# A decoder step's first stage: order of its loads, where x is normalised, which engines split weights, and a shorter block of index queries

## The chip, the core and the metric

The kernel runs on one core of a Trainium2 chip. The core has a matrix engine (TensorE, PE in the profile, with its weight loads as PEld), three engines for elementwise work (VectorE, ScalarE and GpSimd: DVE, ACT and POOL) and SyncE (SP), which here only issues transfers. Each engine runs its own list of instructions in order; they wait for one another through semaphores. Data lies in SBUF (128 partitions) and PSUM (where matmuls accumulate), and comes from HBM by DMA. The metric is the time of one execution on the device in microseconds; less is better.

## The reference

One step of a decoder layer for 1024 new prompt tokens and 8 x 4 sample tokens (32), 1056 columns together, with D = 1024. Cut to what matters:

```python
mod = silu(c) @ w_ada + b_ada                  # (1 + 8 conditions) x 3072
shift, scale, gate = split(mod, 3)
h = x * rsqrt(mean(x*x) + EPS) * g_norm * (1 + scale) + shift
qa, ka, va, za, qi, ki, wi, qr, kr, vr, zr, ga, gr = split(h @ w_in)
# index scores: 4 heads of 64; each query token picks its 256 best keys
s = einsum('bqhd,bsd->bqhs', qi, ki)
scores = einsum('bqhs,bqh->bqs', relu(s), wi * 0.0625)
idx = top_k(where(key <= query, scores, -inf), 256)
y_a = attention of qa over the picked rows of ka, va;  y_a *= silu(za)
y_r = group_norm(retention(rotary(qr), rotary(kr), vr)) * g_ret * silu(zr)
x = x + gate * ((sigmoid(ga) * (y_a @ w_pa) + sigmoid(gr) * (y_r @ w_pr)) @ w_out)
y = rms_norm(x, g_final)
```

The sample tokens see 1024 cached keys, found through a page table, beside their own four. A prompt token below 256 has at most 256 admissible keys, so all of them are taken and its scores decide nothing. The rows of k, v and the index keys and the retention states are outputs too.

## The kernel before, in words

*Numbers.* All products of `h @ w_in` are made in three terms. Each fp32 operand is split in a high part in the reduced format fp32r and the rest: `HH`, `HL` for h, `wh`, `wl` for a weight block. `terms` (L206 to L210) issues, for one row block k of eight and one piece of columns, `wh*HH` (L208), `wh*HL` (L209) and `wl*HH` (L210). The 1056 columns go in three pieces of 352 (`chunks`). A block of 128 output features is thus 3 x 8 x 3 = 72 matmuls.

*Order.* The code is written in a framework that takes each instruction in program order, tracks what it reads and writes, and then orders each engine's list by its own estimates; so work of a later stage may stand among the work of an earlier one. `tc.issue_after(i)` keeps what stands under it behind instruction i. Transfers of SyncE are issued in the order of its list. A pool's `bufs=n` says how many tiles of a name exist; the n+1st waits until the first one is free.

*The head* (L231 to L339) makes HH and HL. The constants C (L146), the 32 sample rows and the eight blocks of 128 rows of x (`x_load`, L253) and the blocks of w_ada (`load_wa`, L320; 16 blocks of 1024 x 128, 512 KB each, in five buffers, a shift and a scale block for each k) come through SyncE. `cond` makes silu(c) transposed. `x_blocks` takes the nine row blocks in three groups of three: sums of squares on ScalarE (L284), an inverse square root by integer start and three Newton steps on VectorE, each x scaled by its factor on VectorE or GpSimd (L291), eight transposes on TensorE (L294) and two copies, one on ScalarE and one on VectorE, into XR, which holds x transposed (L296). `h_tile(k)` then makes shift and scale for 128 features: 2 x 8 small matmuls with the w_ada blocks (`ada_rows`, L198 to L202), a copy (L304), two more small matmuls that add the four partial rows (L307), AA and BB on VectorE (L308, L309), h = XR * AA + BB (L311, the 32 sample columns in two operations at L314), HH as a cast on ScalarE (L315) and HL as the difference, on GpSimd for k = 2, 4, 6 and on VectorE otherwise (L316).

`start_two` (L214 to L226) projects the first two feature blocks, the index keys (KI, with the four index weights behind them) and the first half of the index queries (QI), while HH and HL come: six PSUM banks (2 blocks x 3 pieces) are accumulated over k. Their weights are split on GpSimd (L221, L222).

*Behind the head.* `project` (L356) makes any other block; `prefetch` (L351) loads and splits the next one ahead: cast to wh on ScalarE (L194), wl on GpSimd when the number of blocks left is a multiple of three and on VectorE otherwise (L195). Two buffers each (`wp`). The first prefetched block is the second half of QI. Its results and the first half's go to QS by `use_qi`, those of KI to KH and KL by `use_ki`. The index scores follow: for the row blocks b = 7 down to 2, products of QS with KH and KL (L644, L645), relu on ScalarE (L647), the weighted sum over heads on VectorE (L649, L651) into SC[b]; then the sample rows with gathered cached keys into SCS (L711).

*The selection* (L727 and what follows) searches for each row the threshold of its 256 best keys: VectorE counts entries above a candidate (L727), ScalarE does so for block 7 and the sample rows (L734), and small operations move the candidates (L741 to L747, L803, L805). In the end the picked keys are written as a mask BI (L779 to L783: comparison, running count, choice, mask). Under this stage TensorE makes the retention: for each of four pairs of heads (`pair`) the projections of k, q, v and z, and states S over eight chunks of 128 tokens, seven dependent steps on VectorE (L488), read by TensorE at L507; between the pairs come blocks of the attention queries and of the gates. Then follow the attention keys and values, the attention over masked scores, the output projections and the last norm.

## Time and profile before

| | us |
|---|---|
| median of three runs | 1189.28 (1185.84 to 1189.39) |
| the profiled execution | 1189.59 |
| span in the profile | 1187.8 |
| TensorE busy | 1108.8 (93% of the span), 8040 matmuls |
| VectorE busy | 664.8 (56%) |
| ScalarE busy | 454.3 (38%) |
| GpSimd busy | 329.7 (28%) |
| HBM | 149 GB/s over the span |

A busy time says only that an instruction was under way; which engine sets the time of a stage is told by its waits. A row of the waits names the waiting engine with its tile and line, behind the arrow the engine, tile and line that it waited for, and then the us in all, how many times, and the longest. In a row of the timeline stand start, duration, engine, line, operation, output and inputs with their shapes, and in brackets the idle time before it and what ended it; "x28" means that 28 alike in a row are put together. In a row of the windows stand the length, the busy time (and count) of TensorE's matmuls and weight loads, VectorE, ScalarE and GpSimd, then the granted TensorE clock (1 is full), the mean busy share of the DMA engines and GB/s.

### The profile page before, as it was taken

The page shows a single profiled execution, that of the slowest core. Times are in us where ns is not written, and L with a number is a line of the kernel's source. Part 1 is how long each engine was busy: PE and PEld are TensorE (multiplying, and loading weights), DVE is VectorE, ACT ScalarE, POOL GpSimd, SP SyncE. Part 2 cuts the span into 40 slices and gives each one's busy share as a digit, 9 for nine tenths or more (in the row PEclk, how much of TensorE's full clock was granted, in tenths as well). Part 3 has the DMA queues.
Part 4 walks back from the last instruction along what each step waited for, and adds up shares of the span by engine and source line. Part 5 has one row for each costly group of instructions (what it writes and reads, how often), then busy time and mean ns, then how long its engine had stood idle before and what let it go on. Part 6 is the DMA issues. An engine that isn't in the chain of part 4 may idle for free. (4 is left out here: it accounts for less than half of the span.)

```text
span 1187.8 us, 20303 instructions
## 1 busy us (share of the span) xinstructions
PE 1108.8 (93%) x8040; PEld 1011.9 (85%) x8040; DVE 664.8 (56%) x1599; ACT 454.3 (38%) x874; POOL 329.7 (28%) x258
## 2 busy tenths in 40 slices
PE   4999999999989959999998999999997999988997
PEld 3899989999889959999998999777976888886786
DVE  6765359999999996023222122100364766586655
ACT  5365455554555202122233332211343656432211
POOL 3413016024212511241321212242132333484000
PEclk9899999999999978999999999999998999999999
DMA  9913244144224323332775776687898551586221
GB/s 308 244 35 105 73 122 129 26 151 119 74 78 127 110 57 113 93 106 65 265 252 177 223 215 185 198 287 245 243 246 230 156 159 46 161 248 186 96 104 54
DMA packets 157892, 181.51 MB, mean 153 GB/s; under 512 B 18837, under 2 KB 129501, under 8 KB 156710
## 3 DMA queue, kind: packets, MB, share of 16 engines
q1 hardware_dynamic: 147864, 144.51, 41.5%
q0 software_dynamic: 9856, 35.66, 9.2%
q8 instruction: 63, 1.03, 0.4%
q14 instruction: 31, 0.25, 0.1%
q10 hardware_dynamic: 78, 0.06, 0.0%
HBM read 137.81 MB, written 38.60 MB: 149 GB/s over the span
## 5 line engine op out<-in xcount | busy, mean ns | idle before, releaser
L208 PE MATMUL pj<-hh,wh 128*128 128x352 f32 x1176 | 387.9, 330 | 8.7 <-ACT kx L394 3.7
L210 PE MATMUL pj<-hh,wl 128*128 128x352 f32 x1176 | 382.8, 325 | 0.0
L209 PE MATMUL pj<-hl,wh 128*128 128x352 f32 x1176 | 382.7, 325 | 0.0
L208 PEld LDWEIGHTS pj<-hh,wh 128*128 128x128 f32 x1176 | 223.0, 190 | 18.5 <-issue 6.4
L210 PEld LDWEIGHTS pj<-hh,wl 128*128 128x128 f32 x1176 | 223.2, 190 | 3.9 <-issue 3.4
L209 PEld LDWEIGHTS pj<-hl,wh 128*128 128x128 f32 x1176 | 223.6, 190 | 3.3 <-issue 2.5
L727 DVE TENSOR_SCALAR_CACHE_REDUCE eq<-sc,cand 128x896 bf16<-128x896 f32 (+4 forms) x155 | 135.7, 876 | 2.3
L195 POOL TENSOR_TENSOR wl<-ws,wh 128x1024 fp32r<-128x1024 f32 (+1 forms) x33 | 65.1, 1973 | 187.7 <-ACT wh L194 187.7
L194 ACT CAST wh<-ws 128x1024 fp32r<-128x1024 f32 (+1 forms) x65 | 61.2, 942 | 102.8 <-PE pj L209 66.3
L195 DVE TENSOR_TENSOR wl<-ws,wh 128x1024 fp32r<-128x1024 f32 x32 | 40.0, 1250 | 87.1 <-ACT wh L194 81.2
L1064 POOL TENSOR_SCALAR lg<-lg,st 128x1024 f32<-128x1024 f32 (+7 forms) x64 | 47.4, 746 | 93.4 <-DVE st L1063 83.9
L1062 ACT ACTIVATE lg<-lg,st 128x1024 f32<-128x1024 f32 (+7 forms) x64 | 49.5, 774 | 34.4 <-DVE st L1061 34.1
L734 ACT ACTIVATE ra<-sc,cand 128x1024 bf16<-128x1024 f32 x31 | 35.7, 1151 | 65.1 <-DVE cand L805 65.1
L910 POOL DMA_INDIRECT kv<-in_cache_k,idx x32 | 30.9, 965 | 102.8 <-PE str L940 84.7
L942 DVE COPY kt<-str 128x512 f32<-128x512 f32 x32 | 22.1, 690 | 61.0 <-PE str L940 53.8
L910 POOL DMA_INDIRECT kv<-in_cache_v,idx x32 | 31.7, 992 | 72.4 <-PE sx L968 43.3
L1215 PE MATMUL pj<-woh,MH 128*128 128x512 f32 (+1 forms) x136 | 51.5, 380 | 0.0
L1217 PE MATMUL pj<-woh,ML 128*128 128x512 f32 (+1 forms) x136 | 51.2, 377 | 0.0
L1216 PE MATMUL pj<-wol,MH 128*128 128x512 f32 (+1 forms) x136 | 51.2, 377 | 0.0
L573 ACT ACTIVATE raw<-pj 128x352 f32<-128x352 f32 x48 | 22.1, 460 | 72.5 <-PE pj L210 65.6
L1077 PE MATMUL tr<-C,lg 128*128 128x128 f32 x288 | 43.6, 275 | 0.8 <-DVE pT L1079 0.3
L1057 DVE CUSTOM_DVE_ANT_0 lg<-lg,bi 128x512 f32<-128x512 f32 (+3 forms) x64 | 37.1, 587 | 9.0 <-PE lg L1056 8.4
(337 smaller groups left out, 2054.4 us busy)
## 6 DMA issues: line engine op xcount, KB each, us to landing
ws<-in_w_in SPq DMA_DIRECT2D x51, 512.0 KB
TG<-raw SPq DMA_DIRECT2D x16, 528.0 KB
rot<-in_rot SPq DMA_DIRECT2D x8, 1056.0 KB
wa<-in_w_ada SPq DMA_DIRECT2D x16, 512.0 KB
u<-TG SPq DMA_DIRECT2D x8, 528.0 KB
RT<-u SPq DMA_DIRECT2D x8, 528.0 KB
t<-TG SPq DMA_DIRECT2D x8, 528.0 KB
u<-RT SPq DMA_DIRECT2D x8, 528.0 KB
```

The lines of the kernel that those rows point to most:

```text
L194: nc.scalar.copy(wh[:, :, :n], ws[:, :, :n])
L195: (nc.vector if len(order) % 3 else nc.gpsimd).tensor_sub(wl[:, :, :n], ws[:, :, :n], f32(wh[:, :, :n]))
L208: nc.tensor.matmul(p, wh[:, k], HH[k][:, sl], start=(k == 0), stop=False)
L209: nc.tensor.matmul(p, wh[:, k], HL[k][:, sl], start=False, stop=False)
L210: nc.tensor.matmul(p, wl[:, k], HH[k][:, sl], start=False, stop=(k == KT - 1))
L727: nc.vector.tensor_scalar(junk[:n, :W], sc, thr[:n, j:j + 1], 0.0, op0=op, op1=OP.add, accum_out=cnt[:n, j:j + 1])
L910: nc.gpsimd.indirect_dma_start(out=t.rearrange("p s c -> p (s c)"), out_offset=None, in_=cache.rearrange("g (r s) h d -> (g r) (s h d)", s ...
L1062: nc.scalar.activation(l, l, AF.Exp, bias=st[:, 2:3], scale=0.125, accum_out=st[:, 3:4])
L1064: nc.gpsimd.tensor_scalar(l, l, st[:, 0:1], 0.5, op0=OP.mult, op1=OP.mult)
L1215: nc.tensor.matmul(x, MH[:, k, tk], wh[:, k], start=(k == 0), stop=False)
L1216: nc.tensor.matmul(x, MH[:, k, tk], wl[:, k], start=False, stop=False)
L1217: nc.tensor.matmul(x, ML[:, k, tk], wh[:, k], start=False, stop=(k == KT - 1))
```

## The change

*Loads.* Of C only the first 128 columns, the identity matrix, are loaded first (`C_CAUS` is 128), then the two weight blocks of `start_two`, then x, then the rest of C, then w_ada. The w_ada blocks go into the buffers of the x pool (11 of 4 KB per partition), shift and scale block of a k together. The prefetched w_in blocks stand behind the last w_ada load (`tc.issue_after(loads[-1].ins)`).

*Weights of `start_two`.* They are split by ScalarE (cast) and VectorE (difference) rather than GpSimd. The loop interleaves the banks term by term, and QI has two pieces of 400 columns (256 to 655 and 656 to 1055, `late`) in the place of three of 352; the second half of QI has the same. So there are five banks rather than six.

*x.* `x_block` transposes the raw rows as they come and takes the sum of squares beside it, on VectorE for t = 1 and 4 and on ScalarE otherwise; the squares themselves go into the tile BI[7], which is free then (BI and BIS are allocated earlier for it). `norms` runs for the blocks 0 to 4 and 5 to 8 of SEQ: the inverse square roots, then for each block of 128 tokens a diagonal matrix of them, multiplied with a matrix of ones, which gives each factor in all partitions (RB). The 32 sample columns are scaled at once.

*h.* `modulation` is the first part of the old `h_tile`. AA and the prompt's shift are made on ScalarE, with g_norm * (1 + ...) folded in as scale and bias (`cg`). h = XT * AA * RB in one operation on VectorE; the shift is added in the cast to HH on ScalarE as its bias, and again in the operation that makes HL, which is always on VectorE. The samples' shifts are added before, less the prompt's shift.

GpSimd has no work left in the head, save a share of the low parts of prefetched weights (L195), as before.

```diff
...
-SQD = ()
+SQD = (1, 4)
...
-GRP = (0, 3, 6, 9)
-CP = 0
-PH = (2, 4, 6)
...
-    nc.sync.dma_start(C, A["cst"])
+    nc.sync.dma_start(C[:, :C_CAUS], A["cst"][:, :C_CAUS])
...
+    BI = {b: selp.tile([128, (b + 1) * 128], BF, name=f"bi{b}") for b in range(8)}
+    BIS = selp.tile([NS, LK], BF, name="bis")
...
-            nc.tensor.matmul(x[32 * q:32 * q + 32], scT[:, k], w[:, k], start=(k < 4), stop=(k >= 4))
+            nc.tensor.matmul(x[32 * q:32 * q + 32], scT[:, k], w(k), start=(k < 4), stop=(k >= 4))
...
-    def start_two(pool, f0, f1):
-
-        banks = [pj()[:, :CH] for _ in (0, 1)] + [x[:, o:o + CH] for x in (pl(), pl()) for o in (0, 512)]
-        W = []
-        for f in (f0, f1):
-            ws = wload(wp, w_in, f, 128)
-            wh, wl = [pool.tile([128, KT, 128], F32R, name="x", bufs=9) for _ in "hl"]
-            nc.gpsimd.tensor_scalar(wh, ws, 1.0, 1.0, op0=OP.mult, op1=OP.mult)
-            nc.gpsimd.tensor_sub(wl, ws, f32(wh))
-            W.append((wh, wl))
+    late = [slice(256, 656), slice(656, TT)]
+
+    def start_two(W):
+
+        x, y = pl(), pl()
+        parts_ = [(p[:, :sl.stop - sl.start], sl, i) for p, sl, i in
+                  zip((pj(), pj(), x[:, :512], x[:, 512:], y[:, :512]), chunks + late, (0, 0, 0, 1, 1))]
         for k in range(KT):
-            for i, p in enumerate(banks):
-                terms(p, W[i // 3], k, chunks[i % 3])
-        return banks
+            for term in range(3):
+                for p, sl, i in parts_:
+                    nc.tensor.matmul(p, W[i][term == 2][:, k], (HL if term == 1 else HH)[k][:, sl],
+                                     start=(k == 0 and term == 0), stop=(k == KT - 1 and term == 2))
+        return [p for p, sl, i in parts_]
...
-        NWA = 5
-        warm = sp.tile([1, 1], F32, name="warm")
...
+        ssq = sp.tile([128, 12], F32, name="ssq")
+        nc.vector.memset(ssq, 1.0)
...
+        part = lambda: sp.tile([128, D], F32, name="x", bufs=11)
+        W = []
+        for f in (O_KI, O_QI):
+            ws = wload(wp, w_in, f, 128)
+            wh, wl = [sp.tile([128, KT, 128], F32R, name="w", bufs=4) for _ in "hl"]
+            nc.scalar.copy(wh, ws)
+            nc.vector.tensor_sub(wl, ws, f32(wh))
+            W.append((wh, wl))
+        craw, th = [part()[:9] for _ in (0, 1)]
...
-        rows = sp.tile([48, 128], F32, name="rows")
+        rows = sp.tile([128, 128], F32, name="dg", bufs=3)[:48]
...
+        cg = cols[:, 36:44]
+        one = sp.tile([128, 128], F32, name="one")
+        nc.vector.memset(one, 1.0)
+        XT = sp.tile([128, KT, TT], F32, name="xt")
+        RB = sp.tile([128, TT], F32, name="rb")
...
-            X[t] = sp.tile([128, D], F32, name="x", bufs=9)
-            nc.sync.dma_start(X[t][:n], xp[t * 128:t * 128 + 128] if t < 8 else xs)
+            X[t] = part()
+            nc.sync.dma_start(X[t][:size(t)], xp[t * 128:t * 128 + 128] if t < 8 else xs)
...
+            nc.vector.tensor_tensor(cg, cols[:, 8:16], cols[:, 24:32], op=OP.mult)
...
-        def x_blocks(i0, i1):
...
+        def x_block(i):
+
+            t = SEQ[i]
+            n, x = size(t), X[t]
+            p = pl().rearrange("p (k t) -> p k t", k=KT)
+            for k in range(KT):
+                nc.tensor.transpose(p[:, k, :n], x[:n, 128 * k:128 * k + 128], ident[:n, :n])
+            sq = BI[7]
+            if t in SQD:
+                nc.vector.tensor_tensor_reduce(out=sq[:n], in0=x[:n], in1=x[:n], scale=1.0, scalar=0.0,
+                                               op0=OP.mult, op1=OP.add, accum_out=ssq[:n, i:i + 1])
+            else:
+                nc.scalar.activation(sq[:n], x[:n], AF.Square, accum_out=ssq[:n, i:i + 1])
+            for g, copy in ((slice(0, 4), nc.scalar.copy), (slice(4, 8), nc.vector.tensor_copy)):
+                copy(XT[:, g, t * 128:t * 128 + n], p[:, g, :n])
+
+        def norms(i0, i1):
+
             v = sp.tile([128, i1 - i0], F32, name="vv", bufs=2)
             nc.vector.tensor_scalar(v, ssq[:, i0:i1], 1.0 / D, EPS, op0=OP.mult, op1=OP.add)
             r = rsqrt(sp, v, i1 - i0)
-            for i in range(i0, i1):
-                t = SEQ[i]
-                n, x = size(t), X[t]
-                (nc.vector if t % 2 else nc.gpsimd).tensor_scalar(x[:n], x[:n], r[:n, i - i0:i - i0 + 1], 1.0, op0=OP.mult, op1=OP.mult)
...
-        def h_tile(k, w2):
+            p, c0 = pt(), 128 * SEQ[i1 - 4]
+            for i in range(i1 - 4, i1):
+                dg = sp.tile([128, 128], F32, name="dg", bufs=3)
+                nc.vector.tensor_scalar(dg, ident, r[:, i - i0:i - i0 + 1], None, op0=OP.mult)
+                o = 128 * (i - i1 + 4)
+                nc.tensor.matmul(p[:, o:o + 128], one, dg, start=True, stop=True)
+            nc.scalar.copy(RB[:, c0:c0 + 512], p)
+            if i0 == 0:
+                p = pt()
+                dg = sp.tile([128, 128], F32, name="dg", bufs=3)
+                nc.vector.tensor_scalar(dg[:NS, :NS], ident[:NS, :NS], r[:NS, 0:1], None, op0=OP.mult)
+                nc.tensor.matmul(p[:, :NS], one[:NS], dg[:NS, :NS], start=True, stop=True)
+                nc.vector.tensor_tensor(XT[:, :, T:], XT[:, :, T:], p[:, :NS].unsqueeze(1).to_broadcast([128, KT, NS]), op=OP.mult)
+
+        def modulation(k):
...
-            for o, w in enumerate(w2):
-                ada_rows(pm[:, 128 * o:128 * o + 128], w)
+            for o in (0, 1):
+                ada_rows(pm[:, 128 * o:128 * o + 128], lambda c: wa[k][o][:, c])
...
-            nc.vector.tensor_scalar(AA[:, k], pm[:, 16:25], cols[:, 8 + k:9 + k], cols[:, 24 + k:25 + k], op0=OP.add, op1=OP.mult)
-            nc.vector.tensor_scalar(BB[:, k], pm[:, 0:9], cols[:, k:k + 1], None, op0=OP.add)
...
-            nc.vector.tensor_scalar(h, h, AA[:, k, 0:1], BB[:, k, 0:1], op0=OP.mult, op1=OP.add)
...
-            for op, ab in ((OP.mult, AA), (OP.add, BB)):
-                nc.vector.tensor_tensor(hs, hs, ab[:, k, 1:9].unsqueeze(2).to_broadcast([128, NB, NI]), op=op)
-            nc.scalar.copy(HH[k], XR[:, k])
-            (nc.gpsimd if k in PH else nc.vector).tensor_tensor(HL[k], XR[:, k], f32(HH[k]), op=OP.subtract)
...
-            nc.sync.dma_start(wa[j], wcols(A["w_ada"][0], KT, (j % 2) * 1024 + (j // 2) * 128, 128))
...
+        def h_tile(k, pm):
+
+            shift = BB[:, k, 0:1]
+            nc.scalar.activation(AA[:, k], pm[:, 16:25], AF.Identity, bias=cg[:, k:k + 1], scale=cols[:, 24 + k:25 + k])
+            nc.scalar.activation(shift, pm[:, 0:1], AF.Identity, bias=cols[:, k:k + 1])
+
+            nc.vector.tensor_scalar(BB[:, k, 1:9], pm[:, 1:9], cols[:, k:k + 1], shift, op0=OP.add, op1=OP.subtract)
+            h = XT[:, k]
+            nc.vector.scalar_tensor_tensor(h[:, :T], h[:, :T], AA[:, k, 0:1], RB[:, :T], op0=OP.mult, op1=OP.mult)
+            hs = h[:, T:].rearrange("p (b i) -> p b i", b=NB)
+            by_seq = lambda ab: ab[:, k, 1:9].unsqueeze(2).to_broadcast([128, NB, NI])
+            nc.vector.tensor_tensor(hs, hs, by_seq(AA), op=OP.mult)
+            nc.vector.tensor_tensor(hs, hs, by_seq(BB), op=OP.add)
+            nc.scalar.activation(HH[k], h, AF.Identity, bias=shift)
+            nc.vector.scalar_tensor_tensor(HL[k], h, shift, f32(HH[k]), op0=OP.add, op1=OP.subtract)
+
+        wa, loads = {}, []
+
+        def load_wa(k):
+
+            wa[k] = [part().rearrange("p (k f) -> p k f", f=128) for _ in (0, 1)]
+            for o, w in enumerate(wa[k]):
+                loads.append(nc.sync.dma_start(w, wcols(A["w_ada"][0], KT, 1024 * o + 128 * k, 128)))
...
-        for j in range(NWA - 2):
-            load_wa(j)
-        for i in range(len(GRP) - 1):
-            if i == CP:
-                cond()
-                for j in range(NWA - 2, NWA):
-                    load_wa(j)
-            x_blocks(GRP[i], GRP[i + 1])
+        nc.sync.dma_start(C[:, C_CAUS:], A["cst"][:, C_CAUS:])
+        cond()
+        for i in range(9):
+            x_block(i)
+            if i == 4:
+                norms(0, 5)
+        norms(5, 9)
         for k in range(KT):
-            h_tile(k, (wa.pop(2 * k), wa.pop(2 * k + 1)))
-            for j in (2 * k + NWA, 2 * k + NWA + 1):
-                if j < 16:
-                    load_wa(j)
-        first = start_two(sp, O_KI, O_QI)
+            load_wa(k)
+            h_tile(k, modulation(k))
+        first = start_two(W)
...
-            split.append((f0, wsplit(wp, wload(wp, w_in, f0, 128), 128)))
-
-    def project(f0, use):
+            with tc.issue_after(loads[-1].ins):
+                ws = wload(wp, w_in, f0, 128)
+            split.append((f0, wsplit(wp, ws, 128)))
+
+    def project(f0, use, chunks=chunks):
...
-            p = pj()[:, :CH]
+            p = pj()[:, :sl.stop - sl.start]
...
-                    sl = slice(c * CH, c * CH + CH)
+                    sl = late[c]
...
-                        if c == 2:
+                        if c == 1:
...
-                                                      src[:, CH - NS:].rearrange("p (b i) -> p b i", b=NB))
+                                                      src[:, T - sl.start:].rearrange("p (b i) -> p b i", b=NB))
...
-            project(O_QI + 128, use_qi(2))
+            project(O_QI + 128, use_qi(2), late)
...
```

34 lines of the change are left out of this document (5 added, 29 removed).

## Prediction

> **What bounds the kernel now.** I read the waits of TensorE first, then windows of 40 us, then the waits and the timeline of VectorE, and last the head in windows of 10 us. TensorE is busy in nearly every slice of the page, so the question is where it waits. Between 60 and 820 us one wait stands out (us in total, times, longest):
>
> ```profile
> PE pl L507 <- DVE S L488: 12.2, 1, 12.2
> ```
>
> The windows show why (length, busy us and count of PE, PEld, DVE, ACT, POOL, then clock, DMA share, GB/s); the first and the last of the seven windows of one stage, and the one behind it:
>
> ```profile
> 180.00:220.00 40.00, 37.58 (x271) 35.67 (x270) 38.30 (x90) 21.75 (x40) 16.81 (x9) 0.96 0.36 108
> ...
> 420.00:460.00 40.00, 27.82 (x187) 26.85 (x186) 38.92 (x58) 4.57 (x9) 0.56 (x1) 0.70 0.18 49
> 460.00:500.00 40.00, 40.00 (x255) 39.72 (x254) 7.78 (x19) 8.51 (x14) 7.43 (x4) 1.00 0.44 131
> ```
>
> From 180 to 460 us VectorE is full (38.3 and 38.9 of 40 us; 7.8 in the next): it searches the thresholds of the top keys (L727 and what follows), and TensorE, which fills the time with projections, runs out of work at 426 and stands still until VectorE has written S for the third pair of retention heads. So up to 438.7 us the path is: head, projections and index scores on TensorE, then VectorE's queue. From there TensorE is again nearly always busy, and the end follows it. VectorE becomes full when ScalarE has counted its first row block:
>
> ```profile
> DVE base L747 <- ACT ra L734: 6.4, 2, 5.9
> ```
>
> ```profile
> 161.61 1.00 ACT L711 COPY scs<-pl 32x1024 f32<-32x1024 f32 x1 [2.65 <-PE pl L709]
> ```
>
> This wait ends at 163.8 us: ScalarE stood until L709 on TensorE had finished. The start of VectorE's stage thus hangs on TensorE's queue, and TensorE's queue on the head:
>
> ```profile
> 36.98 0.92 PE L208 MATMUL pj<-hh,x 128*128 128x352 f32 x2 [1.33 <-ACT hh L315]
> ...
> 43.78 0.33 PE L209 MATMUL pl<-hl,x 128*128 128x352 f32 x1
> ...
> 70.26 0.32 PE L210 MATMUL pl<-hh,x 128*128 128x352 f32 x1
> ```
>
> The first product of the head's projection stands at 36.98; its last (L210 on pl) starts at 70.26 and starts follow each other by 0.16 us, so it ends at 70.4. Up to 43.8 the same products run at about half speed.
>
> **Part by part.** *Index queries from token 256 on.* Each of two column blocks gets 2 pieces of 400 columns for 3 of 352. One block is 72 products before (3 pieces x 8 x 3 terms) and 48 after. TensorE's timeline gives the prices, at half clock behind the long wait and at full clock later:
>
> ```profile
> 438.66 3.25 PE L507 MATMUL pl<-S,qrT 64*128 64x64 f32 x28 [12.18 <-DVE S L488]
> ...
> 449.57 0.49 PE L210 MATMUL pj<-hh,wl 128*128 128x352 f32 x1
> 449.86 0.49 PE L208 MATMUL pj<-hh,wh 128*128 128x352 f32 x1
> ...
> 453.38 0.32 PE L208 MATMUL pj<-hh,wh 128*128 128x352 f32 x1
> 453.54 0.32 PE L209 MATMUL pj<-hl,wh 128*128 128x352 f32 x1
> ```
>
> Full clock: 453.54 - 453.38 = 0.16 us for 352 columns, so 0.182 for 400. 72 x 0.16 = 11.5 and 48 x 0.182 = 8.7: 2.8 us less for the second block, all of it on TensorE's queue ahead of L709. The first block's part lies in the head.
>
> *Order of the projections among the index scores.* The built programs show 301 projection products between the second query block and the last L709 before (144 of the head and 72 of that block not counted) and 278 after. 23 x 0.16 = 3.7 us less stand ahead of VectorE's full stage; they are done behind it, where TensorE has the 12.2 us of slack.
>
> *VectorE's order in front of S.* In the changed program seven operations of the selection have moved ahead of the sixth S step of the third pair (L516 there), which is what TensorE waits for. Their prices stand in the timeline, where they now come behind that step (438.23):
>
> ```profile
> 438.23 0.28 DVE L488 SCALAR_TENSOR_TENSOR S<-S,rc,pt 128x64 f32<-128x64 f32 x1
> ...
> 438.42 0.76 DVE L782 SCALAR_TENSOR_TENSOR ra<-sc,base,ra 128x512 f32<-128x512 f32 x1
> ...
> 439.08 0.56 DVE L779 TENSOR_SCALAR eq<-sc,base 128x640 f32<-128x640 f32 x1
> ...
> 440.17 0.43 DVE L783 TENSOR_SCALAR bi<-ra 128x512 bf16<-128x512 f32 x1
> ...
> 440.63 1.49 DVE L780 TENSOR_TENSOR_SCAN ra<-eq 128x640 f32<-128x640 f32 x1
> ...
> 442.16 0.88 DVE L781 SCALAR_TENSOR_TENSOR ra<-ra,rem,eq 128x640 f32<-128x640 f32 x1
> ...
> 443.08 0.89 DVE L782 SCALAR_TENSOR_TENSOR ra<-sc,base,ra 128x640 f32<-128x640 f32 x1
> ...
> 443.88 0.61 DVE L779 TENSOR_SCALAR eq<-sc,base 128x768 f32<-128x768 f32 x1
> ```
>
> 0.76 + 0.56 + 0.43 + 1.49 + 0.88 + 0.89 + 0.61 = 5.6 us later for S. VectorE has no idle time there to hide them.
>
> *First weights first, w_ada and prefetches last.* SyncE's queue now issues 64 KB of C, two 512 KB blocks of w_in, x, the rest of C, all sixteen w_ada blocks, and only then the prefetched w_in blocks (the new wait of prefetch on the last w_ada load) and ptab. Before, the third w_in block went out behind nine w_ada blocks. On ScalarE the cast of that prefetched block (L193) stands behind the third HH and ahead of AA for k = 3. What waits there: AA, the next sum, HH 3 to 7, and through them VectorE's h and HL and TensorE. Bytes ahead of and in that block: 0.07 + 1.05 + 4.33 + 0.34 + 16 x 0.524 + 0.52 = 14.70 MB. What the transfers moved:
>
> ```profile
> 0.00:10.00 10.00, 0.00 (x0) 0.00 (x0) 1.02 (x7) 4.74 (x7) 0.20 (x4) 1.00 0.82 281
> 10.00:20.00 10.00, 5.29 (x32) 4.95 (x33) 8.52 (x33) 8.57 (x18) 3.67 (x3) 1.00 1.10 350
> 20.00:30.00 10.00, 7.31 (x105) 5.71 (x104) 9.65 (x22) 3.31 (x7) 6.53 (x5) 1.00 1.18 292
> 30.00:40.00 10.00, 8.12 (x112) 6.81 (x111) 9.55 (x18) 5.71 (x9) 4.36 (x4) 0.85 1.14 287
> 40.00:50.00 10.00, 10.00 (x93) 9.26 (x90) 8.86 (x11) 2.83 (x4) 5.27 (x2) 0.81 1.13 291
> ```
>
> 10 us at 281, 350, 292, 287 and 291 GB/s sum to 2.8, 6.3, 9.2, 12.1 and 15.0 MB, so 14.70 MB are moved by 48.9 us. The lag from there to landing, and when ScalarE reaches the cast, come from these rows:
>
> ```profile
> 31.30 1.69 SPq L188 DMA_DIRECT2D ws<-in_w_in  x1
> ...
> 38.51 1.05 ACT L194 CAST wh<-ws 128x1024 fp32r<-128x1024 f32 x1 [0.44 <-DMA ws<-in_w_in]
> ...
> 39.47 1.07 ACT L315 CAST hh<-xr 128x1056 fp32r<-128x1056 f32 x1
> ...
> 39.64 3.23 POOL L195 TENSOR_TENSOR wl<-ws,wh 128x1024 fp32r<-128x1024 f32 x1 [5.56 <-ACT wh L194]
> ...
> 40.70 2.21 DVE L314 TENSOR_TENSOR xr<-xr,AA 128x32 f32<-128x32 f32 x1
> ```
>
> The block issued at 31.30 held bytes 10.5 to 11.0 MB; 11.0 MB are moved at 36.3 and the cast that waited 0.44 us for it started at 38.51, so landing comes 2.1 us later: 51.0 us after the change. ScalarE reaches that cast behind its third HH, which started at 39.47 before. In the new head the last x lands at about 19.6 us (5.44 MB, same sums); transposes, sums of squares and copies go by arrival, and the norm factors, one broadcast and one h_tile of 1.3 + 0.6 + 1.1 + 1.3 us follow, so the third HH ends near 40 too. ScalarE therefore stands about 11 us, and TensorE from about 48 on.
>
> The rate is not one number: 350 GB/s while x came in rows of 4 KB (10 to 20 us), 287 to 292 with w_ada and w_in in rows of 512 B. I go by these windows. The Trainium skill, DMA: Bandwidth & Descriptors, Specifications, puts the least transfer for full line rate at 512 B; by that the narrow rows would run like the wide ones, and here the trace disagrees.
>
> *From that landing to the end of the head's projection.* Prices:
>
> ```profile
> L202 PE MATMUL pt<-wa,scT 128*32 128x128 f32 x256 | 9.9, 286 | 0.0
> ...
> L315 ACT CAST hh<-xr 128x1056 fp32r<-128x1056 f32 x8 | 8.6, 1075 | 11.6 <-DVE xr L314 9.8 <-DVE xr L311 1.8
> ...
> L195 POOL TENSOR_TENSOR wl<-ws,wh 128x1024 fp32r<-128x1024 f32 x2 | 5.6, 2804 | 5.9 <-ACT wh L194 5.9
> ...
> L651 DVE SCALAR_TENSOR_TENSOR sc<-rl,wsc,sc 128x1024 f32<-128x1024 f32 x3 | 3.8, 1279 | 1.5 <-ACT rl L647 1.4
> ...
> L194 ACT CAST wh<-ws 128x1024 fp32r<-128x1024 f32 x4 | 4.2, 1049 | 1.4 <-PE pj L209 0.9 <-DMA ws<-in_w_in 0.4
> ...
> L195 DVE TENSOR_TENSOR wl<-ws,wh 128x1024 fp32r<-128x1024 f32 x2 | 2.5, 1226 | 0.5 <-ACT wh L194 0.5
> ...
> L316 DVE TENSOR_TENSOR hl<-xr,hh 128x1056 fp32r<-128x1056 f32 x5 | 6.3, 1255 | 3.4 <-ACT hh L315 3.4
> ...
> L309 DVE TENSOR_SCALAR BB<-pt,cols 128x9 f32<-128x9 f32 x8 | 1.8, 219 | 0.0
> ```
>
> Count from the landing. Cast 1.05; its low part goes to GpSimd, done at +3.5 (two of mean 2.80, one was 3.23, so 2.38 alone). While GpSimd holds it VectorE's SBUF work waits (39.64 + 3.23: the 32-column L314 took 2.21 us). So the 1024-wide product of h for k = 3 (as L651, 1.28) ends at +4.8, two short ones of 0.2, the second prefetch's low part 1.23 and one more short at +6.6; HH 1.08 at +7.8; HL 1.26 at +9.1. TensorE has stood over 5 us by then and is taken at half clock: 15 products of k = 3 at 0.29 to 0.33, then a modulation of 32 x 0.034 = 1.1, whose copy ScalarE's queue holds ahead of HH 4: HH 4 ends at +15.7, HH 5 at +16.8, HL 5 at +18.3. AA 7 waits on TensorE for the first five products of k = 5: +20.6. Then h 1.28, HL 6 1.26, HH 7 1.08, HL 7 1.26 and 0.7 of short ones: +26.2; ten products of 0.17 behind: +28. So 51 + 28 = 79 us for 70.4 before: 8.6 us later. Lower end: no block by GpSimd and full clock throughout, +24, so 4.6 later; upper end: half clock to the end, +33, so 13.6.
>
> On the clock the trace has two cases: 6.8 us at half (36.98 to 43.8), and 14.7 us after the 12.18 us wait (438.66 to 453.4). I take the first, since the gap is shorter. The Trainium skill, TensorE: Matmul & The Clock Gate, Part 1, says one window of about 3.4 us of work suffices; with 3.4 us the count would come some 1.5 us lower.
>
> *The rest of the head.* Raw transposes, norm broadcast by 9 small products, AA and HH with bias, sums of squares in BI, the end of GpSimd's scaling and splitting: all ahead of 40 us, covered by the transfers, since x and w_ada arrive at the same rate whatever the engines do; without that cover the serial chain of 4.2 us per k is what they would cost. ptab goes out some 10 us later; its gather (79.1 us before) has room.
>
> **Sum.** +8.6 - 2.8 - 3.7 = +2.1 at VectorE's stage, +5.6 at S: +7.7 at 438.7, and the same to the end, as TensorE arrives at S at 426.5 + 8.6 - 2.8 = 432, before S at 446. The profiled execution took 1189.59 us (span 1187.8), 0.3 above the median 1189.28: 1189.6 + 7.7 = 1197.3, beside the median 1197.0.
>
> **Rivals.** *The cast does not hold the head* (faster). If the prefetched block lands before ScalarE gets there, the chain runs on at VectorE's and ScalarE's pace: 40.4 + 5.5 for k = 3 + 2 x 7.4 for the last pairs + 1.7 = 62.5, 7.9 earlier; -7.9 - 6.5 + 5.6 = -8.8: 1180.8. It decides at a landing by 40.4 us, so 420 GB/s from 10 us on, where the windows had 287 to 350. For it: only VectorE's gain by no longer waiting for GpSimd, as it did with the 2.21 us, so the chain may be shorter and the queue's order matter less. 0.17.
> *The narrow rows run like the wide ones* (same). At 350 GB/s from 10 us on, 14.70 MB are moved at 44.0 and the block lands at 46.1, 4.9 us sooner: +7.7 - 4.9 = +2.8: 1192.1. For it, less data competes at the head now; against it, three windows in a row at 287 to 292. 0.05. (By the rule of the skill cited above.)
> *The tail is short* (same): GpSimd holds nothing, the clock recovers at once, and the landing is 1.5 us sooner: 4.6 - 1.5 - 6.5 + 5.6 = +2.2: 1191.5. For it: GpSimd's work is only 2.4 us. 0.07.
> *The clock stays low* (slower still): +13.6 - 6.5 + 5.6 = +12.7: 1202.3. For it, the 14.7 us case. 0.13.
>
> **How the numbers follow.** Forecast 0.58, the rest as given. The forecast's own range is 1192.5 to 1200.5. The stated range, 1185 to 1204, takes in the two cases without a clear change, and leaves out most of the faster case and the far end of the slow one, some 2 in 10 together. A change under 0.3% (3.6 us) cannot be told from none. Slower: 0.58 + 0.13 = 0.71; same 0.05 + 0.07 = 0.12; faster 0.17.
>
> **What would show it.** Right: ScalarE idle about 11 us before L193 with the transfer of ws as releaser; TensorE nearly idle near 48 to 56 us and its clock at half behind it; the head's last product near 79; VectorE full from about 166; TensorE's wait for S still there, some 14 us, ending near 446. Wrong: the cast waits under 3 us; S does not end TensorE's wait, or comes at 438 or earlier though the head is late; or the two parts cancel against another wait behind 460 us.

## The result and the profile after

The changed kernel takes 1199.46 us in the median (1196.41 to 1200.05) for 1189.0 of the kernel before: 1.0089 times as long, with a 95% interval of 1.0064 to 1.0113. It is slower by about 10.5 us; the forecast was 1197.0. The profiled execution is the fastest of them: 1196.41 us with a span of 1194.6, so it shows 6.8 of the 10.5 us.

Where the time went is best seen between five marks on TensorE: the end of the head (where the first transpose of `kiT` starts), the end of the last L709 (L735 in the changed kernel), and its reads of S (L507, now L535) for the first three pairs. The stretch between the first two marks is called the index stage below. Windows of the kernel before, with the columns of the prediction's windows:

```profile
0.00:70.42 70.42, 51.15 (x513) 46.46 (x514) 45.29 (x107) 31.68 (x53) 24.94 (x17) 0.95 0.85 235
70.42:161.57 91.15, 90.33 (x560) 79.73 (x558) 45.64 (x86) 48.98 (x84) 13.97 (x11) 1.00 0.25 74
161.57:224.07 62.50, 60.08 (x410) 57.95 (x410) 56.42 (x141) 35.16 (x63) 19.83 (x10) 0.97 0.41 119
224.07:324.23 100.16, 96.70 (x701) 93.03 (x700) 94.80 (x252) 55.21 (x97) 26.52 (x13) 1.00 0.36 104
324.23:438.66 114.43, 97.49 (x698) 94.27 (x698) 110.38 (x233) 43.31 (x77) 32.45 (x14) 0.94 0.33 96
438.66:750.54 311.88, 307.90 (x2323) 293.74 (x2323) 92.54 (x168) 86.86 (x169) 78.02 (x58) 0.97 0.53 164
```

The same windows of the changed kernel:

```profile
0.00:79.71 79.71, 55.12 (x508) 47.34 (x508) 45.41 (x103) 35.43 (x67) 2.52 (x5) 0.89 0.74 206
79.71:166.58 86.87, 85.16 (x513) 73.54 (x512) 43.44 (x82) 44.98 (x76) 11.73 (x10) 1.00 0.32 90
166.58:233.17 66.59, 64.00 (x439) 60.98 (x438) 61.30 (x147) 37.75 (x68) 22.51 (x11) 1.00 0.34 97
233.17:340.02 106.85, 99.13 (x695) 95.02 (x694) 102.73 (x267) 56.60 (x100) 26.87 (x13) 0.97 0.33 98
340.02:451.89 111.87, 97.64 (x701) 94.78 (x701) 107.75 (x219) 41.22 (x74) 32.59 (x14) 0.95 0.34 99
451.89:760.74 308.85, 306.68 (x2321) 292.51 (x2321) 87.47 (x161) 86.51 (x168) 78.00 (x58) 0.98 0.54 166
```

The head is 9.3 us longer, the index stage 4.3 shorter, the way to the first read of S 4.1 longer (3.9 of it TensorE's work), that to the second 6.7 longer, that to the third 2.6 shorter: S is read 13.2 us later. Between the first and the second read TensorE has no more work than before (695 for 701), but idles 7.7 us for 3.5 and has a clock of 0.97 for 1.00, and VectorE is busy 7.9 us longer. Behind the third read 3.0 us come back by 760, and 3.4 later.

In the head, ScalarE's timeline (the third HH, and what follows):

```profile
43.95 1.18 ACT L342 ACTIVATE hh<-xt,BB 128x1056 fp32r<-128x1056 f32 x1 [2.33 <-DVE xt L341]
51.32 1.04 ACT L193 CAST wh<-ws 128x1024 fp32r<-128x1024 f32 x1 [6.19 <-DMA ws<-in_w_in]
52.27 0.35 ACT L332 ACTIVATE AA<-pt,cols 128x9 f32<-128x9 f32 x1
```

The cast of the prefetched block waits 6.19 us for its transfer, and AA for k = 3 stands behind it. TensorE's idle time and clock follow, in windows of 10 us:

```profile
40.00:50.00 10.00, 8.50 (x100) 7.11 (x99) 4.32 (x6) 2.73 (x5) 0.00 (x0) 1.00 1.08 277
50.00:60.00 10.00, 4.25 (x40) 3.59 (x41) 6.04 (x7) 4.61 (x9) 2.34 (x1) 0.55 0.52 138
60.00:70.00 10.00, 9.45 (x97) 8.39 (x97) 6.12 (x12) 3.69 (x8) 0.00 (x0) 0.77 0.05 16
```

And its longest waits from 60 to 820 us:

```profile
PE pl L535 <- DVE S L516: 11.8, 1, 11.8
PE pj L207 <- ACT qs L424: 5.3, 2, 2.8
PE pl L557 <- DVE ss L554: 2.7, 1, 2.7
```

The wait for S is still there and hardly shorter; the one for `ss` (L526 of the kernel before) is new.

### The profile page after: what moved, and what is told of

It reads as the page before. It is cut to its first block, busy times and chain, and to the rows that moved or that the text cites. A ratio compares the mean times of both kernels' runs of the same rounds, so it can differ in the third digit from the quotient of the medians.

```text
span 1194.6 us, 20246 instructions
## 1 busy us (share of the span) xinstructions
PE 1111.3 (93%) x8010; PEld 1009.7 (85%) x8010; DVE 665.9 (56%) x1591; ACT 455.2 (38%) x882; POOL 307.1 (26%) x246
## 5 line engine op out<-in xcount | busy, mean ns | idle before, releaser
L207 PE MATMUL pj<-hh,wh 128*128 128x352 f32 (+1 forms) x1168 | 384.6, 329 | 10.4 <-ACT qs L424 5.3
L209 PE MATMUL pj<-hh,wl 128*128 128x352 f32 (+1 forms) x1168 | 381.8, 327 | 0.0
L208 PE MATMUL pj<-hl,wh 128*128 128x352 f32 (+1 forms) x1168 | 380.8, 326 | 0.0
L194 POOL TENSOR_TENSOR wl<-ws,wh 128x1024 fp32r<-128x1024 f32 (+1 forms) x33 | 62.3, 1889 | 207.7 <-ACT wh L193 207.7
```

The costliest lines, as they stand in the source:

```text
L194: (nc.vector if len(order) % 3 else nc.gpsimd).tensor_sub(wl[:, :, :n], ws[:, :, :n], f32(wh[:, :, :n]))
L207: nc.tensor.matmul(p, wh[:, k], HH[k][:, sl], start=(k == 0), stop=False)
L208: nc.tensor.matmul(p, wh[:, k], HL[k][:, sl], start=False, stop=False)
L209: nc.tensor.matmul(p, wl[:, k], HH[k][:, sl], start=False, stop=(k == KT - 1))
```

## The experiments

Theory A, from the prediction: the head stands at a cast whose block lands late, and the delay runs on to the end. Theory B, from the windows above: the lists behind the head are in another order, and that is where the time goes. A third, that the seven selection operations in front of S cost their 5.6 us, is tested apart. Ratios are to the kernel before, measured beside each run; its median there was 1187.6 to 1190.3, so a difference in us between two runs can be off by 1 to 2 us for that alone.

**The casts behind the eighth HH.**

```diff
-            nc.scalar.activation(HH[k], h, AF.Identity, bias=shift)
+            casts.append(nc.scalar.activation(HH[k], h, AF.Identity, bias=shift))
...
-            split.append((f0, wsplit(wp, ws, 128)))
+            with tc.issue_after(casts[-1].ins): split.append((f0, wsplit(wp, ws, 128)))
```

> The changed kernel, with ScalarE's casts of the prefetched weight blocks placed behind the eighth HH; transfers as in the changed kernel. Theory (ScalarE stood before the cast of a block that landed at 51 us, and the head stood with it): ScalarE has no wait of over 3 us between the third and the eighth HH. HH 1, 2 and 3 started 4.35 us apart in the changed kernel (35.26, 39.61, 43.95), so the eighth starts at 65.7 at the latest and the head's last product ends between 63 and 70 instead of 79.7, 10 to 17 us earlier; VectorE's order ahead of S is not touched, so the sum is about 1187 (1183 to 1191). Rival (the head waits for its w_ada blocks, which land as late as before, or for VectorE; the cast only uses idle time): the head still ends at 77 or later and the time stays at 1196 to 1202.

Measured: 1198.89 us, 1.0075 (1.0053 to 1.0098), for 1.0089 of the changed kernel: no clear change, and far from the 1187 expected. Yet the head ends at 68.1, 11.6 us earlier: the stall is real. Most of the gain (7.3 of the 11.6 us) goes at once, as the two casts and the low part now stand in front of the copies of KI and QI, and TensorE waits 5.2 us for them and falls to half clock for a time. In the timeline:

```profile
64.81 1.99 ACT L193 CAST wh<-ws 128x1024 fp32r<-128x1024 f32 x2
...
66.83 2.76 DVE L194 TENSOR_TENSOR wl<-ws,wh 128x1024 fp32r<-128x1024 f32 x1 [0.57 <-ACT wh L193]
```

In the waits of TensorE:

```profile
PE pl L670 <- DVE qs L635: 5.2, 1, 5.2
```

And in the window of the index stage:

```profile
68.12:162.29 94.17, 88.42 (x513) 76.19 (x512) 45.21 (x84) 45.05 (x76) 12.13 (x11) 0.95 0.32 94
```

The same 513 matmuls take 94.17 us for 86.87. So the cast must stand somewhere else, not just later.

**No wait on the last w_ada load.**

```diff
-            with tc.issue_after(loads[-1].ins):
+            if True:
```

> The changed kernel without the wait of the prefetched blocks on the last w_ada load; two of them then go out behind the first and the second w_ada block, a third and a fourth between the later ones, and the first two casts stand ahead of the first modulation. Theory (as above: where the cast stands against the landing of its block): the blocks land by about 28 us, ScalarE waits little, but 14 w_ada blocks come up to 3.6 us later (two blocks of 1.05 MB at 290 GB/s); head's end 66 to 73, sum about 1189 (1185 to 1193). Rival (the head waits for w_ada): the head is later than in the run with the late casts by the full 3.6 us or more, and not much earlier than 79.7.

1191.66 us, 1.0018 (0.9996 to 1.004). The head ends at 74.5, the index stage takes 85.5, S is read at 444.5. The first two casts stand at 26.8 us without a wait. Theory A holds here: the new wait, with the place of the cast, is worth some 8 of the 10.5 us. The way from the first read of S to the second is still 106.7 us.

**The end of the selection behind S, in the changed kernel and in the kernel before.**

```diff
-            nc.vector.scalar_tensor_tensor(S[:, c], S[:, c - 1], ...
+            step[p, c] = nc.vector.scalar_tensor_tensor(S[:, c], S[:, c - 1], ...
...
-                nc.vector.tensor_scalar(eq[:n, :W], sc, t, None, op0=OP.is_equal)
+                with tc.issue_after(step[2, 6].ins) if 512 <= W <= 896 else nullcontext(): nc.vector.tensor_scalar(eq[:n, :W], sc, t, None, op0=OP.is_equal)
```

> The changed kernel, with the end of the selection for the blocks of 512 to 896 columns placed behind the sixth S step of the third pair on VectorE; the head is as in the changed kernel. Theory (TensorE's wait of 11.8 us ends with that step, and the operations that moved ahead of it cost 5.6 us there): S comes 7 to 9 us earlier (the 512 and part of the 640 block), at about 443.5 instead of 451.9; TensorE arrives at 440, so its wait falls to 3 or 4 us; the time falls by 6 to 9 us, to about 1192. Rival (the wait is only where a later limit shows, and what is gained there is lost behind it, as VectorE must still do the same operations): the wait falls, and the time stays within 2 us of 1199.

> The kernel before with the same order: the end of the selection from the block of 512 columns on behind the sixth S step of the third pair. Six operations (0.35 + 0.48 + 1.22 + 0.75 + 0.75 + 0.55 = 4.1 us by the timeline) leave the way of S. Theory: S at 434.5 instead of 438.7, the time 4 us lower, about 1185. Rival (TensorE's wait there costs nothing in the end): 1189 as before.

1197.5 us, 1.0066 (1.0045 to 1.0087), and 1188.55, 0.9999 (0.9979 to 1.0019). Neither time differs clearly from that of its kernel without the edit. In the first S is read at 446.6, 5.3 us earlier, with 15 of the selection's operations ahead of it for 25, but the wait is still 9.1: the framework's planner also put fewer products ahead of the read. The last window before it:

```profile
341.60:446.64 105.04, 93.61 (x677) 90.76 (x676) 100.84 (x209) 40.24 (x72) 32.60 (x14) 0.96 0.35 105
```

677 matmuls for 701; those left out are done behind it. In the kernel before S is read 1.8 us earlier, with no measurable gain. Both rivals were nearer: what S gains is mostly work moved behind it.

**The casts behind the fifth and the sixth HH; all else behind the head in the order of the changed kernel.**

```diff
+            with tc.issue_after(casts[4 if f0 == O_QI + 128 else 5].ins): split.append((f0, wsplit(wp, ws, 128)))
```

> The changed kernel with the first two prefetched blocks' casts placed behind the fifth and the sixth HH, where the blocks have landed (51 and 53 us) and well ahead of the head's end. Behind the head all lists of instructions are those of the changed kernel. The run with the casts behind the eighth HH had its head end 11.6 us earlier, but stood 5.2 us and ran at half clock soon after it, as the casts and their low parts were in front of the copies of KI and QI. Theory (the head's stall carries the loss; the casts only must not stand elsewhere): the head's last product ends at 69 to 72 instead of 79.7, TensorE idles under 2 us between there and the last index product, VectorE's stage starts at 158 to 161; S of the third pair, 13 us late in the changed kernel, comes 8 to 10 us earlier; the time is 1190 (1187 to 1193). Rival (the order behind the head makes the loss, as the time did not move when the head got shorter): TensorE's idle time and lost clock behind the head grow by what the head gains, and the time stays at 1196 or more.

1195.0 us, 1.0039 (1.0027 to 1.0051): half of what was expected. The head ends at 77.3 only. Two things hold it up. TensorE ran at half clock when the first products began, without a cause in its list, which up to there is that of the run with the casts behind the eighth HH. That run's window of 30 to 40 us, and then this one's:

```profile
30.00:40.00 10.00, 8.13 (x106) 6.57 (x109) 4.79 (x9) 4.22 (x10) 0.00 (x0) 1.00 1.16 288
```

```profile
30.00:40.00 10.00, 9.04 (x85) 6.65 (x86) 3.77 (x6) 3.66 (x9) 0.00 (x0) 0.50 1.19 288
```

And the low part of the block on GpSimd held VectorE up, in the timeline:

```profile
57.91 2.60 POOL L194 TENSOR_TENSOR wl<-ws,wh 128x1024 fp32r<-128x1024 f32 x1 [57.48 <-ACT wh L193]
58.17 3.43 DVE L337 SCALAR_TENSOR_TENSOR xt<-xt,AA,rb 128x1024 f32<-128x1024 f32 x1
```

L337 takes 1.28 us elsewhere. Theory A is right in kind; on this evidence the stall is worth 4.5 to 8 us. But S is still read 9.6 us later than before, while the last L735 ends 1.2 later.

**One round of the search behind the first pair's `ss`, without and with the casts in the middle.** What the pairs' steps stand behind can be counted in VectorE's list: the rounds of the search, one new candidate each. Groups of the candidates' line from the start of VectorE's stage to the sixth S step of the second pair, before (window 163.7 to 323.4) and after (168.7 to 339.3):

```profile
L805 DVE TENSOR_SCALAR cand<-base 128x7 int32<-128x7 int32 x21 | 5.7, 273 | 0.5
```

```profile
L831 DVE TENSOR_SCALAR cand<-base 128x7 int32<-128x7 int32 x23 | 13.1, 569 | 0.6
```

21 and 23; with the first candidate, which has a line of its own, 22 and 24, and so counted the first pair's `ss` has 9 and 11 ahead of it. A round takes 5.4 us where little else stands in it (in the changed kernel 237.67 to 243.10, from candidate to candidate). What that does to the first `ss` (before, then after; TensorE's product and VectorE's answer):

```profile
229.49 0.25 PE L524 MATMUL pl<-qrT,krT 64*32 64x32 f32 x4
230.77 0.20 DVE L526 TENSOR_TENSOR ss<-pl,dm 32x64 f32<-32x64 f32 x1
```

```profile
238.59 0.25 PE L552 MATMUL pl<-qrT,krT 64*32 64x32 f32 x4
244.71 0.20 DVE L554 TENSOR_TENSOR ss<-pl,dm 32x64 f32<-32x64 f32 x1
244.97 1.50 PE L557 MATMUL pl<-st,qm 64*32 64x64 f32 x32 [2.73 <-DVE ss L554]
```

From the product to the answer it takes 1.3 us before, 6.1 after. The edit puts the tenth round behind it:

```diff
-        nc.vector.tensor_tensor(ss.rearrange("p (i t) -> p i t", i=2), px[:NS]...
+        step[p] = nc.vector.tensor_tensor(ss.rearrange("p (i t) -> p i t", i=2), px[:NS]...
...
-                count(cand.bitcast(F32))
+                with tc.issue_after(step[0].ins) if k == 21 else nullcontext(): count(cand.bitcast(F32))
```

> The kernel of the run with the casts behind the fifth and sixth HH, and besides the tenth round of the search (counts with the ninth moved candidate) behind the first pair's step ss (L554) on VectorE. In the changed kernel ss stood behind ten moved candidates and TensorE waited 2.7 us for it, in the kernel before it stood behind eight. Theory (the order puts more of the search in front of the first pair's steps; this costs idle time of 4.2 us and lost clock of 3.4 us between the reads of S of the first and the second pair): these fall to 3.5 and 0 to 1.7 as before, S of the third pair comes 2 to 5 us earlier than in the run without it, and the time is 1 to 5 us lower, 1185 to 1189. Rival (what TensorE gains there it loses again at the wait for S of the third pair, which VectorE's amount of work sets): that wait grows by as much and the time is that of the other run within 1 us.

> The changed kernel with its head as it is, and the tenth round of the search behind the first pair's ss on VectorE; VectorE's list then has 9 and 22 moved candidates ahead of the sixth S step of the first and second pair and 10 ahead of the first ss, as in the run with the two edits; the changed kernel has 9, 24 and 11, the kernel before 8, 22 and 9. Theory (two shares add up: the head, and the rounds of the search ahead of the pairs' steps): of the 16 us between the changed kernel and the run with both edits, the casts gave 4.5 (1195.0) and the order 11.5; so 1188 (1185 to 1191). Rival (the order only helps once the head is shorter): 1194 or more.

With the casts in the middle: 1183.51 us, 0.9939 (0.9917 to 0.9962), 11.5 us below the same head without it and faster than the kernel before. With the head as it is: 1192.72, 1.0038 (1.0014 to 1.0062), 6.7 us below the changed kernel, though above the range that was expected. The windows from the first to the second and on to the third read of S, of the latter:

```profile
233.12:335.19 102.07, 97.78 (x703) 93.76 (x702) 96.16 (x254) 54.09 (x96) 27.43 (x13) 1.00 0.36 102
335.19:443.07 107.88, 94.86 (x691) 91.64 (x691) 105.07 (x227) 42.17 (x77) 29.45 (x14) 0.98 0.35 102
```

The first is back at 102.1 us and full clock, the second does not give it away, and S is read 8.8 us earlier than in the changed kernel. So theory B holds beside A, and the rival (the wait for S takes it back) falls: that wait is 8.8 us here, for 11.8. How much the new order is worth depends on the head it stands behind, 6.7 or 11.5 us. S comes 8.8 us earlier in both, so the difference arises behind it; why stays open.

The edit does not change the one round alone, since the planner writes the whole list anew: the third pair's sixth step now has 20 operations of the selection ahead of it for 25. The first window, 4.8 us shorter, lies ahead of all that. The 4.0 us of the second cannot be laid to the round alone; the run with 15 such operations was 2.0 us faster than the changed kernel.

**Both causes removed: no wait on w_ada, and the round behind `ss`.**

> Both causes removed in the way that was the best for each: the prefetched blocks go out among the w_ada loads (no wait on the last of them; 1191.7 alone), and the tenth round stands behind the first ss (11.5 us less on the other head). Theory (they add up): 1180 (1177 to 1184), clearly below the kernel before and at or below the run with casts behind the fifth and sixth HH. Rival (TensorE's wait for S of the third pair takes back what the head gains, as VectorE's list is the limit there): that wait grows to 12 us or more and the time is 1184 to 1187.

1186.54 us, 0.9965 (0.9945 to 0.9985): 12.9 us below the changed kernel, where the two edits alone gave 7.8 and 6.7: within the intervals they add up. My 1180 had taken the 11.5 for the order. The time is the rival's (1184 to 1187), but not by its cause: the wait for S fell from 12.1 to 10.8 us, where growth to 12 or more was its sign. From the first to the second read of S, without the round's edit and with it:

```profile
227.54:334.21 106.67, 97.82 (x694) 93.60 (x693) 102.61 (x267) 56.56 (x100) 26.82 (x13) 0.98 0.32 98
```

```profile
227.40:329.66 102.26, 97.53 (x703) 93.41 (x702) 96.33 (x257) 54.46 (x98) 26.86 (x13) 1.00 0.35 102
```

**The index queries from 256 alone, in the kernel before.** `late`, `start_two`, `project` and `use_qi` as in the change, all else as before.

> The kernel before with the index queries from token 256 on alone (two pieces of 400 columns for three of 352 in both blocks). TensorE has 48 products less of 352 columns and 0.16 us (72 x 0.16 = 11.5 against 48 x 0.182 = 8.7, twice): 5.6 us less work, 2.8 of it behind the head. Theory: the start of VectorE's stage comes 3 to 6 us earlier, S as much unless the order in front of it changes, and the time falls by 2 to 5 us, to 1184 to 1187. Rival (less work on TensorE only lengthens its wait for S, and the reordered lists decide): the time stays within 2 us of the kernel before or rises, with TensorE's idle time and lost clock up by as much as its work is down.

1182.82 us, 0.9933 (0.9909 to 0.9956), 7.5 us less than its kernel before, by the interval 5.2 to 10.8: the 5.6 us of work, and perhaps more. The last L709 ends at 154.1, 7.5 earlier; S is read 2.8 earlier and the rest comes behind it. VectorE's list has 9, 23 and 10 candidates ahead of the first and second pair's S and the first `ss`, halfway to the changed kernel: the shorter queries alone bring some of the disorder.

**The same with the round behind `ss`.** The edit of above in the kernel of the last run.

> The kernel before with the shorter index queries alone, and the tenth round of the search behind the first ss. Without the second edit it has 9, 23 and 10 moved candidates ahead of the three steps, and 7.1 us of idle time on TensorE between the reads of S of the first and second pair, against 3.5 in the kernel before. Theory: idle time there back at 3 to 4 us, time 2 to 4 us below 1182.8: 1179 to 1181. Rival (with one round more or less it is no matter, the two-round step made the difference): 1182 to 1184.

1176.13 us, 0.9872 (0.9844 to 0.9901): the best kernel, 1.3% below the kernel before and 6.7 us below the run without the edit. The two windows up to the third read of S:

```profile
221.00:321.11 100.11, 97.43 (x696) 93.88 (x695) 94.59 (x252) 53.49 (x95) 26.56 (x13) 0.98 0.36 104
321.11:428.72 107.61, 99.73 (x714) 96.91 (x713) 104.56 (x228) 43.80 (x78) 30.30 (x14) 0.97 0.36 103
```

100.1 us again as in the kernel before, and 107.6 for 114.4. The first `ss` has ten candidates ahead of it with the edit and without; with it the second pair's sixth step has 22 for 23, the third's 15 operations of the selection for 17. So here too the edit's 6.7 us are those of a whole new list. TensorE's longest wait is no longer for S, but 7.9 us for `raw` (L392 on VectorE), with products still ahead of the read. The kernel before with this edit alone was not run.

**The new wait alone, in the kernel before.**

```diff
-            nc.sync.dma_start(wa[j], wcols(A["w_ada"][0], KT, ...))
+            loads.append(nc.sync.dma_start(wa[j], wcols(A["w_ada"][0], KT, ...)))
...
+            with tc.issue_after(loads[-1].ins): split.append((f0, wsplit(wp, wload(wp, w_in, f0, 128), 128)))
```

> The kernel before with the one new wait: the prefetched blocks behind the last w_ada load. The lists put their casts behind the fifth and sixth HH there (in the kernel before behind the second and the fourth). Theory: 16 w_ada blocks come 1.8 us or more earlier for it, the prefetched blocks land at about 50 us, ScalarE reaches the first cast at about that time and stands under 4 us; the head's end stays within 3 us of 70.4 and the time within 4 us of 1189.5: the wait costs by where the cast stands, not by itself. Rival (behind all of w_ada the blocks are late in any head): ScalarE stands over 5 us before a cast and the time rises to 1194 or more.

1187.5 us, 0.9978 (0.9955 to 1.0): no loss. The planner put the casts later in ScalarE's list there:

```profile
47.02 1.07 ACT L315 CAST hh<-xr 128x1056 fp32r<-128x1056 f32 x1 [1.67 <-DVE xr L314]
51.09 1.05 ACT L194 CAST wh<-ws 128x1024 fp32r<-128x1024 f32 x1 [3.00 <-DMA ws<-in_w_in]
```

The block lands as late, but ScalarE stands only 3 us and the head ends at 67.5. The wait costs by where its cast stands.

**The first two weight blocks split on GpSimd, in the changed kernel.** L240 and L241 on GpSimd.

> The changed kernel with the two weight blocks of start_two split on GpSimd, as before, and not on ScalarE and VectorE; the order of all else is the same. Theory (which engine splits them costs nothing, since x arrives until 20 us and the head waits for the prefetched block until 51): the first product of the head within 1 us of 36.6, its last within 2 us of 79.7, the time within 2 us of 1199.5. Rival (the split on ScalarE and VectorE delays the sums of squares and copies of x, and with them all that follows): the first product comes 2 us or more earlier and the time falls by that. Third (GpSimd's work holds VectorE up where both use SBUF, as in the head before): the first product comes later and the time rises by 2 us or more.

1198.44 us, 1.0079 (1.0054 to 1.0105); head's end 78.9. As expected, which engine splits them does not show.

## Why the prediction held, point by point

*The path.* Right: S for the third pair still ends TensorE's long wait (11.8 us), VectorE is full in front of it, and the change is slower by more than the 0.3% below which the prediction sees no difference. The sum was +7.7. In the profiles the head gave +9.3 for +8.6, the index stage -4.3 for -6.5, the way from there to S +8.2 for +5.6, and what lies behind S -6.4 for nothing: +13.2 at S, +6.8 in the end, +10.5 between the medians. That the forecast came out near is in part luck: errors of both signs met.

*The late block.* The transfer's sum held: 51.0 forecast, the cast ran at 51.32. ScalarE got there at 45.1 and not at 40, since the three HH follow each other by 4.35 us (35.26, 39.61, 43.95), so it stood 6.2 and not 11 us. In the new order TensorE makes the next modulation behind the products of this k, and ScalarE's AA behind its HH; that serial chain was counted too short. The end of the head needed 28.4 us from the landing for 28: 79.7 for 79. The clock took the worse of the two cases: half clock for (0.45 + 0.23) x 10 / 0.5 = 13.6 us between 50 and 70, where 6.8 was taken, so the rest of the tail must have taken less than was counted. That 28 came out is luck in this part.

*The rival that the cast does not hold the head* had 1180.8. With the cast out of the way the head ended at 68.1, not 62.5 (its terms add up to 62.4), and 1191.7 was the best time by that alone. Of the rivals' times 1180.8 and 1202.3 start from 1189.6, the other two from the median 1189.28. The old head with the shorter queries ends at 68.9 and 68.0 in the two kernels that have it: the new head, its stall aside, is no faster than the old one.

*The rates.* The narrow rows stayed slow: 277 to 292 GB/s for w_ada, and 393 while x came. The Trainium skill, DMA: Bandwidth & Descriptors, Specifications, has the full rate from 512 B on; the trace disagrees here as it did before.

*The shorter queries and the moved products.* The index stage was to lose 6.5 us and lost 4.3: TensorE's work there fell by 5.2, and 0.9 of new idle time came. The step that failed is "they are done behind it, where TensorE has the 12.2 us of slack": the 23 products were done ahead of the first read of S (3.9 us more work in that window), and no slack paid for them there. For the queries the sum has 2.8 us; alone, in the old head, they gave 7.5 (5.2 to 10.8), where their work in the head, another 2.8, counts too.

*The order in front of S.* Counted as 5.6 us. From the start of its stage to the read of S VectorE took 283.1 us for 274.9, 8.2 longer. But the runs with that order undone gave 2.0 and 1.0 us of time: the step that a later S is paid one for one fails. What the runs showed in its place is the order ahead of the first and second pair's steps: two further rounds of the search stand there. Lists with the tenth round behind `ss` were faster by 5.1 to 11.5 us in four pairs of runs. The window from the first to the second read of S, where the edit acts first, shrank by 3.3 to 5.3 us in them; the rest comes behind it, where the list changed too. The same comparison of the two lists, done only in front of the last S, was not done for the earlier pairs.

*"The same to the end".* Wrong in the profile: 6.4 us came back behind S. Much of that may belong to this one execution, 3.1 us below its median: from S to the end it took 742.7 us, the eight other runs with the new head 744.5 to 750.4, and the kernel before 749.1. In the runs with the shorter queries the window from S to 750 or so is about 3 us shorter; its cause was not looked into.

## What to carry to other kernels

Where a planner writes each engine's list, a change of one stage reorders later ones: compare the lists in front of every wait, not only the longest, and count the rounds of the saturated engine ahead of each step that another engine waits for. A load that is put last needs its consumer put late as well, but not so late that it stands in front of the next stage's copies. An earlier end of a wait is worth little where the waiting engine's own work has only been moved behind it: S came 5.3 us earlier, with 24 fewer products ahead of it, and the time fell by 2.0.

## What was not expected of the hardware

The same list of TensorE ran its first products at a clock of 1.00 in one kernel and of 0.50 in another, busy for 8.13 and 9.04 of 10 us (the two windows shown above). The Trainium skill, TensorE: Matmul & The Clock Gate, Part 1, lets one window of about 3.4 us of work suffice and says that the windows run freely. The trace does not agree that one busy window is enough: in the second kernel TensorE was busy for all 6.80 us from 37.05 to 43.85, at a clock of 0.50. Nor was it an accident of one execution: the kernel with the same head and the round behind `ss`, measured on the same device, has 9.04 us and 0.50 from 30 to 40 us again. What decides it stays open.

VectorE's L337 took 3.43 us for 1.28 while GpSimd's 2.60 us operation ran. The Trainium skill, SBUF — State Buffer, Terms, calls the port pair of the two an exclusive lock that is held for the full instruction; the 2.15 us agree. The candidates' line has a mean of 569 ns for 273 in the longer search, and the trace shows the same beside it: five of the 23 took 0.67 to 2.37 us, each with an instruction of GpSimd under way (at 199.29 us 2.37, beside one of 2.47 that had begun at 199.16), the others 0.16 to 0.17. This does not explain the longer way from the first to the second read of S: in the two windows of 106.67 and 102.26 us above, two candidates each were held up so, for 2.32 to 2.34 us.
